# A gated linear unit in float32: two-row tiles in two slots, or one-row tiles in six

## The chip, the cores and the metric

The kernel runs on one core of a Trainium2 chip. A core has a matrix engine (TensorE, not used here), VectorE (DVE), ScalarE (ACT), GpSimd (POOL) and SyncE (SP), a scratch memory (SBUF) of 128 partitions, and 16 DMA engines that carry data between SBUF and the chip's main memory (HBM). DMAs are issued here from two queues: the loads from SP, the stores from ACT. The metric is the device time of one execution in microseconds; a kernel is run several times and the median counts. The profile is of one further execution.

## The reference

```python
def setup_inputs():
    return {"x": np.random.randn(8192, 8192).astype(np.float32)}

def reference(x):
    a, b = np.split(x, 2, axis=-1)
    return a * (1 / (1 + np.exp(-b)))
```

Each row of 8192 numbers (32 KiB) is cut into a front half `a` and a back half `b` of 4096 each. The output row is `a * sigmoid(b)`, 4096 numbers (16 KiB). So 268.4 MB are read, 134.2 MB are written, and each output needs one sigmoid and one product.

## The kernel before

A tile is 128 partitions with two rows each: 64 KiB in and 32 KiB out for each partition, 8 MiB and 4 MiB in all, and 32 tiles cover the input. In HBM, four neighbouring rows belong to one partition: two of them go with an even tile, the other two with the odd tile that follows (`"(g p h r) m -> g h p (r m)"`). A partition's share of a tile is thus one contiguous run, and the runs of two neighbouring partitions start 128 KiB apart in the input and 64 KiB in the output.

SBUF holds two input buffers `x_sb` and two output buffers `o_sb`; tile i uses those of number i % 2.

The work on a tile goes in this order:

1. `load(i)` (line 63) issues the load on SP. It waits for the multiplications of tile i - 2, which read that buffer.
2. `work` (lines 82 to 84) runs the sigmoid on ACT, in place over the back halves, and then the product into `o_sb`. A tile in the middle is cut into two pieces by columns: the first 768 columns of both rows (the list `few_and_most`) are multiplied on POOL, the other 3328 on DVE. The first and the last tile are cut into four pieces, all multiplied on DVE.
3. `store(i)` (line 68) issues the store on ACT, behind the sigmoids, and waits for the products. Before ACT begins the sigmoid of tile i, it also waits until the store of tile i - 2 has landed, because that store frees the output buffer (`by_sigmoid`).

After the work on tile i the program issues the load of tile i + 2 and then the store of tile i. The first tile is loaded and stored in two rows, so that work can begin early; the last one is stored in three pieces.

Each instruction passes through `place`, which keeps the program's order on its engine and drops every dependency except those it is given. Tile's framework adds one kind of wait of its own: DMAs take eight semaphores in turn, and a DMA waits until the earlier one on its semaphore has landed.

Two functions rewrite the finished program at its ends. `_launch_early` puts the first load ahead of the start barrier. `_close_on_sync` lets SP wait for the last store while POOL clears the semaphores. The change leaves both as they are.

Of the kernel before, what the change touches and what calls it, by code (L numbers as in the profile page):

```python
# [8 lines left out]
def _tiles(ctx, tc, x, out):  # L9
    nc = tc.nc  # L10
    P = nc.NUM_PARTITIONS
    DEP = mybir.DependencyInfo(mybir.DependencyClass.Sync, mybir.DependencyReason.DATA)
    fp32 = mybir.dt.float32
    SIG = mybir.ActivationFunctionType.Sigmoid

    n_rows, n_cols = x.shape
    half = n_cols // 2
    R = 2
    SLOTS = 2
    n_tiles = n_rows // (P * R)  # L20
    x_g = x.rearrange("(g p h r) m -> g h p (r m)", p=P, h=2, r=R)
    out_g = out.rearrange("(g p h r) m -> g h p (r m)", p=P, h=2, r=R)

    pool = ctx.enter_context(tc.tile_pool(name="io", bufs=1))
    xs = [pool.tile([P, R * n_cols], fp32, name=f"x_sb{k}") for k in range(SLOTS)]
    os = [pool.tile([P, R * half], fp32, name=f"o_sb{k}") for k in range(SLOTS)]

    whole = [(0, 8)]
    rows = [(0, 4), (4, 8)]
    cut = half // 16 * 3  # L30
    few_and_most = [(0, 8, 0, cut), (0, 8, cut, half)]
    fourths = [(k, k + 2, k % 4 * half // 4, (k % 4 + 2) * half // 4) for k in range(0, 8, 2)]
    loads = [whole] * n_tiles
    works = [few_and_most] * n_tiles
    stores = [whole] * n_tiles
    behind = [0] * n_tiles
    loads[0] = stores[0] = rows
    works[0] = works[-1] = fourths
    stores[-1] = [(0, 4), (4, 6), (6, 8)]
    behind[-1] = 1  # L40

    def meet(a, b):
        return a[0] < b[1] and b[0] < a[1]

    traced = [[] for _ in range(SLOTS)]
    load_of, mul_of, store_of = {}, {}, {}

    def place(i, ins, *needs):


        kept = {n.ins.name for n in needs}
        for e in traced[i % SLOTS]:
            if e.ins.name not in kept:
                tc.declare_no_dep(ins.ins, e.ins, reason="follows from the waits that are kept")
        traced[i % SLOTS].append(ins)
        tc.keep_in_program_order(ins)
        return ins

    def load(i):
        for lo, hi in loads[i]:  # L60
            c = slice(lo * n_cols // 4, hi * n_cols // 4)
            free = [m for w, m in mul_of.get(i - SLOTS, []) if meet(w, (lo, hi))]
            ins = nc.sync.dma_start(out=xs[i % SLOTS][:, c], in_=x_g[i // 2, i % 2, :, c])  # L63
            load_of.setdefault(i, []).append(((lo, hi), place(i, ins, *free)))

    def store(i, lo, hi):
        c = slice(lo * half // 4, hi * half // 4)
        ins = nc.scalar.dma_start(out=out_g[i // 2, i % 2, :, c], in_=os[i % SLOTS][:, c])  # L68
        done = [m for w, m in mul_of[i] if meet(w, (lo, hi))]
        store_of.setdefault(i, []).append(((lo, hi), place(i, ins, *done)))  # L70

    def work(i, lo, hi, near, far):

        rows = xs[i % SLOTS].rearrange("p (r h m) -> p r h m", r=R, h=2)
        packed = os[i % SLOTS].rearrange("p (r m) -> p r m", r=R)
        r, c = slice(lo // 4, (hi + 3) // 4), slice(near, far)
        b = rows[:, r, 1, c]
        landed = [s for w, s in load_of[i] if meet(w, (lo, hi))]
        gone = [s for w, s in store_of.get(i - SLOTS, []) if meet(w, (lo, hi))]
        by_sigmoid = 0 < i < n_tiles - 1  # L80
        needs = [*landed, *(gone if by_sigmoid else ())]
        sig = place(i, nc.scalar.activation(out=b, in_=b, func=SIG), *needs)  # L82
        engine = nc.gpsimd if far == cut and i > 1 else nc.vector
        mul = engine.tensor_mul(out=packed[:, r, c], in0=rows[:, r, 0, c], in1=b)  # L84
        if by_sigmoid:
            for s in gone:
                tc.add_manual_dep(sig.ins, s.ins.name, DEP, reason="frees the output slot")
        place(i, mul, sig, *(() if by_sigmoid else gone))
        mul_of.setdefault(i, []).append(((lo, hi), mul))

    for i in range(SLOTS):
        load(i)
    for i in range(n_tiles):
        due = list(stores[i])
        for k, piece in enumerate(works[i]):
            work(i, *piece)
            ready = works[i][k - behind[i]][1] if k >= behind[i] else 0
            while len(stores[i]) > 1 and k < len(works[i]) - 1 and due[0][1] <= ready:
                store(i, *due.pop(0))
        if i + SLOTS < n_tiles:  # L100
            load(i + SLOTS)
        for lo, hi in due:
            store(i, lo, hi)


def _launch_early(nc):
# [68 lines left out]
@with_exitstack  # L175
def kernel(
    ctx: ExitStack,
    tc: tile.TileContext,
    x: bass.AP,
    out: bass.AP,  # L180
):
    nc = tc.nc
    with ExitStack() as pools:
        _tiles(pools, tc, x, out)
    tc.close()
    tc.compile()
    _launch_early(nc)
    _close_on_sync(nc)
# [30 lines left out]
```

## Time and profile before

| | |
|---|---|
| runs | 932.68 us median of 3 (932.6 to 932.75) |
| the profiled execution's span | 931.1 us |
| loads | 33 DMAs: 31 of 8 MiB, 2 of 4 MiB |
| stores | 35 DMAs: 30 of 4 MiB, 3 of 2 MiB, 2 of 1 MiB |
| from issue to landing, median | 43.5 us for a load, 43.6 us for a store |
| ACT waits for stores to land (line 82) | 630.0 us in 29 waits |
| SP waits for DVE's products (line 63) | 855.5 us in 30 waits |

The span is the profile's time from the first instruction to the end of the last transfer; what a run takes beyond it lies around the program. In the lines of the profile, `q1` is the queue of the loads and `q10` that of the stores; behind the name stand packets, megabytes and the share of the 16 DMA engines' time. A row of the timeline has start, duration, engine, line, operation, output and input, and in brackets how long the engine had been idle and who ended that. A group of instructions has its count, the busy microseconds, the mean nanoseconds of one, and the idle time before.

### The profile page before, as it was taken

To read this page: it belongs to the slowest core of one execution; us is meant where nothing else is said; L and a number is where in the kernel's file an instruction comes from. 1 tells how busy PE (TensorE), PEld (TensorE's weight loads), DVE (VectorE), ACT (ScalarE), POOL (GpSimd) and SP (SyncE) were. 2 spreads that over 40 slices of the span, in tenths; PEclk is the share of its full clock that TensorE was granted. 3 is DMA by queue.
4 is the path that set the end of the run, shared out by engine and by line. 5 is a ranking of instruction groups with operands and counts; after the bars stand their busy time and mean duration, and the time that the engine had idled before them with its cause. 6 is when DMAs were issued, how large, how long until landed. Compare 5 with 4: busy or idle time off the path is not lost.

```text
span 931.1 us, 325 instructions
## 1 busy us (share of the span) xinstructions
DVE 232.5 (25%) x39; ACT 229.8 (25%) x69; POOL 99.9 (11%) x33
## 2 busy tenths in 40 slices
DVE  1133311333113331133320333203332033320233
ACT  2123332033320333203332023320233302333023
POOL 0001111011110111101111011110111101111010
DMA  9999999999999999999999999999999999999998
GB/s 405 450 439 417 428 450 424 455 405 428 450 428 450 407 469 409 428 450 427 452 405 450 428 428 450 424 452 408 428 450 428 450 408 465 411 428 450 427 452 383
DMA packets 9793, 402.67 MB, mean 432 GB/s; under 512 B 1088, under 2 KB 1088, under 8 KB 1088
## 3 DMA queue, kind: packets, MB, share of 16 engines
q1 hardware_dynamic: 4752, 268.44, 66.6%
q10 hardware_dynamic: 5040, 134.22, 33.4%
q14 instruction: 1, 0.01, 0.0%
HBM read 268.44 MB, written 134.22 MB: 432 GB/s over the span
## 4 chain that ended last, share of the span: by engine, by line
DMA 75%; DVE 12%; ACT 12%; issue 0%; ACTq 0%; SPq 0%
DMA out_dram<-o_sb 65%; DVE o_sb L84 12%; ACT x_sb L82 12%; DMA x_sb<-in_x_dram 10%; ACTq L68 0%; SPq L63 0%
## 5 line engine op out<-in xcount | busy, mean ns | idle before, releaser
L84 DVE TENSOR_TENSOR o_sb<-x_sb 128x6656 f32<-128x6656 f32 (+2 forms) x39 | 232.5, 5970 | 690.2 <-ACT x_sb L82 690.2
L82 ACT ACTIVATE x_sb<-x_sb 128x1536 f32<-128x1536 f32 (+1 forms) x68 | 228.5, 3407 | 689.9 <-DMA out_dram<-o_sb 630.0
L84 POOL TENSOR_TENSOR o_sb<-x_sb 128x1536 f32<-128x1536 f32 x29 | 99.7, 3437 | 787.7 <-ACT x_sb L82 787.7
L82 ACT ACT_TABLE_LOAD x1 | 1.3, 1283 | 0.8 <-PEq L203 0.8
L203 POOL MEMSET const-float32-0.0<- 128x1 f32 x1 | 0.1, 98 | 0.2 <-issue 0.2
L203 POOL MEMSET const-bfloat16-1.0<- 128x1 bf16 x1 | 0.1, 101 | 0.0
L203 POOL MEMSET const-uint8-127<- 128x1 uint8 x1 | 0.1, 101 | 0.0
L203 POOL MEMSET const-float32-1.0<- 128x1 f32 x1 | 0.1, 98 | 0.0
## 6 DMA issues: line engine op xcount, KB each, us to landing
out_dram<-o_sb ACTq DMA_DIRECT2D x30, 4096.0 KB, 43.6
x_sb<-in_x_dram SPq DMA_DIRECT2D x2, 4096.0 KB, 16.4
out_dram<-o_sb ACTq DMA_DIRECT2D x3, 2048.0 KB, 28.0
out_dram<-o_sb ACTq DMA_DIRECT2D x2, 1024.0 KB, 8.3
x_sb<-in_x_dram SPq DMA_DIRECT2D x31, 43.5
```

The lines of the kernel that those rows point to most:

```text
L82: sig = place(i, nc.scalar.activation(out=b, in_=b, func=SIG), *needs)
L84: mul = engine.tensor_mul(out=packed[:, r, c], in0=rows[:, r, 0, c], in1=b)
L203: nc = _bacc.Bacc("TRN2", target_bir_lowering=False, num_devices=1)
```

## The change

A tile becomes one row for each partition: 64 tiles with 32 KiB in and 16 KiB out for each partition. Four neighbouring rows still belong to one partition; they now go to four tiles that follow each other. There are six slots of 32 KiB for each partition and no output buffers: the product overwrites the front half of the tile, and the store reads it there. A slot is therefore free when its store has landed, and `load(i)` waits for the store of tile i - 6. DVE does all the products. A tile is one sigmoid, one product and one store; the first and the last tile are cut into two halves by columns, each with a store of its own. Six loads are placed ahead of the first work. The first load is as large as before (4 MiB), but is now the whole first tile.

```diff
-    R = 2
-    SLOTS = 2
-    n_tiles = n_rows // (P * R)
-    x_g = x.rearrange("(g p h r) m -> g h p (r m)", p=P, h=2, r=R)
-    out_g = out.rearrange("(g p h r) m -> g h p (r m)", p=P, h=2, r=R)
+    SLOTS = 6
+    n_tiles = n_rows // P
+    x_g = x.rearrange("(g p r) m -> g r p m", p=P, r=4)
+    out_g = out.rearrange("(g p r) m -> g r p m", p=P, r=4)
...
-    xs = [pool.tile([P, R * n_cols], fp32, name=f"x_sb{k}") for k in range(SLOTS)]
-    os = [pool.tile([P, R * half], fp32, name=f"o_sb{k}") for k in range(SLOTS)]
+    xs = [pool.tile([P, n_cols], fp32, name=f"x_sb{k}") for k in range(SLOTS)]
...
+    ends = {0, n_tiles - 1}
...
     def load(i):
-        for lo, hi in loads[i]:
-            c = slice(lo * n_cols // 4, hi * n_cols // 4)
-            free = [m for w, m in mul_of.get(i - SLOTS, []) if meet(w, (lo, hi))]
-            ins = nc.sync.dma_start(out=xs[i % SLOTS][:, c], in_=x_g[i // 2, i % 2, :, c])
-            load_of.setdefault(i, []).append(((lo, hi), place(i, ins, *free)))
+        ins = nc.sync.dma_start(out=xs[i % SLOTS], in_=x_g[i // 4, i % 4])
+        load_of[i] = place(i, ins, *store_of.get(i - SLOTS, ()))
...
-    def work(i, lo, hi, near, far):
+    def work(i, near, far):
...
-        engine = nc.gpsimd if far == cut and i > 1 else nc.vector
-        mul = engine.tensor_mul(out=packed[:, r, c], in0=rows[:, r, 0, c], in1=b)
...
+        a = xs[i % SLOTS][:, near:far]
+        b = xs[i % SLOTS][:, half + near : half + far]
+        sig = place(i, nc.scalar.activation(out=b, in_=b, func=SIG), load_of[i])
+        mul = place(i, nc.vector.tensor_mul(out=a, in0=a, in1=b), sig)
+        ins = nc.scalar.dma_start(out=out_g[i // 4, i % 4, :, near:far], in_=a)
+        store_of.setdefault(i, []).append(place(i, ins, mul))
+
+    def pieces(i):
+        return [(0, half // 2), (half // 2, half)] if i in ends else [(0, half)]
 
     for i in range(SLOTS):
         load(i)
     for i in range(n_tiles):
-        due = list(stores[i])
-        for k, piece in enumerate(works[i]):
+        for piece in pieces(i):
             work(i, *piece)
...
         if i + SLOTS < n_tiles:
             load(i + SLOTS)
-        for lo, hi in due:
-            store(i, lo, hi)
```

More of the change, by code (lines that the diff above doesn't have):

```diff
@@ L17, in _tiles @@
     half = n_cols // 2
-    R = 2
-    SLOTS = 2
-    n_tiles = n_rows // (P * R)
-    x_g = x.rearrange("(g p h r) m -> g h p (r m)", p=P, h=2, r=R)
-    out_g = out.rearrange("(g p h r) m -> g h p (r m)", p=P, h=2, r=R)
-    pool = ctx.enter_context(tc.tile_pool(name="io", bufs=1))
-    xs = [pool.tile([P, R * n_cols], fp32, name=f"x_sb{k}") for k in range(SLOTS)]
-    os = [pool.tile([P, R * half], fp32, name=f"o_sb{k}") for k in range(SLOTS)]
[L28 to L43, printed above, removed]
+    SLOTS = 6
+    n_tiles = n_rows // P
+    x_g = x.rearrange("(g p r) m -> g r p m", p=P, r=4)
+    out_g = out.rearrange("(g p r) m -> g r p m", p=P, r=4)
+    pool = ctx.enter_context(tc.tile_pool(name="io", bufs=1))
+    xs = [pool.tile([P, n_cols], fp32, name=f"x_sb{k}") for k in range(SLOTS)]
+    ends = {0, n_tiles - 1}
     traced = [[] for _ in range(SLOTS)]
-    load_of, mul_of, store_of = {}, {}, {}
+    load_of, store_of = {}, {}
     def place(i, ins, *needs):
@@ L59, in load @@
     def load(i):
-        for lo, hi in loads[i]:
-            c = slice(lo * n_cols // 4, hi * n_cols // 4)
-            free = [m for w, m in mul_of.get(i - SLOTS, []) if meet(w, (lo, hi))]
-            ins = nc.sync.dma_start(out=xs[i % SLOTS][:, c], in_=x_g[i // 2, i % 2, :, c])
-            load_of.setdefault(i, []).append(((lo, hi), place(i, ins, *free)))
[L66 to L70, printed above, removed]
-    def work(i, lo, hi, near, far):
[L74 to L82, printed above, removed]
-        engine = nc.gpsimd if far == cut and i > 1 else nc.vector
[L84 to L89, printed above, removed]
+        ins = nc.sync.dma_start(out=xs[i % SLOTS], in_=x_g[i // 4, i % 4])
[9 more added lines that the diff above has]
+        return [(0, half // 2), (half // 2, half)] if i in ends else [(0, half)]
     for i in range(SLOTS):
@@ L93, in _tiles @@
     for i in range(n_tiles):
-        due = list(stores[i])
-        for k, piece in enumerate(works[i]):
+        for piece in pieces(i):
             work(i, *piece)
-            ready = works[i][k - behind[i]][1] if k >= behind[i] else 0
-            while len(stores[i]) > 1 and k < len(works[i]) - 1 and due[0][1] <= ready:
-                store(i, *due.pop(0))
         if i + SLOTS < n_tiles:
             load(i + SLOTS)
-        for lo, hi in due:
-            store(i, lo, hi)
 def _launch_early(nc):
```

## The prediction

> **What bounds the kernel now.** I read the page first, its slices and queues, then the queues again for three stretches of the span.
>
> ```profile
> span 931.1 us, 325 instructions
> DVE 232.5 (25%) x39; ACT 229.8 (25%) x69; POOL 99.9 (11%) x33
> ...
> DMA  9999999999999999999999999999999999999998
> ...
> HBM read 268.44 MB, written 134.22 MB: 432 GB/s over the span
> ...
> DMA out_dram<-o_sb 65%; DVE o_sb L84 12%; ACT x_sb L82 12%; DMA x_sb<-in_x_dram 10%; ACTq L68 0%; SPq L63 0%
> ```
>
> No engine is busy for more than a quarter of the span; the transfers are, in every slice. The chain of waits charges 24% to DVE and ACT. That is misleading: it names who released whom, and while DVE multiplies tile i the 16 DMA engines carry other tiles. What counts is whether they ever pause. So the queues, from 100 to 883 us (27 tiles), from 3 to 11 us (loads of one row alone) and from 24 to 45 us (64 KiB load packets beside 16 KiB store packets):
>
> ```profile
> DMA packets 7777, 339.75 MB, mean 434 GB/s; under 512 B 864, under 2 KB 864, under 8 KB 864
> ...
> q1 hardware_dynamic: 3888, 226.49, 66.7%
> q10 hardware_dynamic: 3888, 113.25, 33.5%
> ```
> ```profile
> q1 hardware_dynamic: 102, 3.34, 96.7%
> ```
> ```profile
> q1 hardware_dynamic: 112, 7.34, 81.0%
> q10 hardware_dynamic: 108, 1.77, 19.6%
> ```
>
> In the steady stretch the shares add to 100.2%: the DMA engines never rest, and neighbouring packets overlap by a hair. A packet is one partition's contiguous run: 31 of the 33 loads give 128 of 64 KiB each. Leaving out 432 semaphore packets per queue (864 under 512 B), 3456 loads took 66.7% of 16 x 783 us, 2.418 us each, and the stores of 32 KiB 1.214 us. From the second stretch a 32 KiB load packet takes 0.967 x 8 x 16 / 102 = 1.213 us, from the third a 16 KiB store packet 0.196 x 21 x 16 / 108 = 0.610 us. So 32 KiB more cost 1.205 us (27.2 GB/s for one engine, 435.1 for 16), and every packet has about 8 ns on top, of which some 4 ns overlap with its neighbour (the 0.2%). At 435.1 GB/s all 402.65 MB take 925.4 us. The span is 5.7 us longer: start, packet costs and end are all there is to win.
>
> Last, the work of one tile in the timeline and the shapes of the instructions:
>
> ```profile
> 99.66 7.12 ACT L82 ACTIVATE x_sb<-x_sb 128x1536 f32<-128x1536 f32 x2 [21.82 <-DMA out_dram<-o_sb]
> 101.22 3.44 POOL L84 TENSOR_TENSOR o_sb<-x_sb 128x1536 f32<-128x1536 f32 x1 [25.51 <-ACT x_sb L82]
> 106.81 7.09 DVE L84 TENSOR_TENSOR o_sb<-x_sb 128x6656 f32<-128x6656 f32 x1 [21.85 <-ACT x_sb L82]
> 113.99 0.35 ACTq L68 DMA_DIRECT2D out_dram<-o_sb  x1
> 128.66 7.12 ACT L82 ACTIVATE x_sb<-x_sb 128x1536 f32<-128x1536 f32 x2 [21.88 <-DMA out_dram<-o_sb]
> ```
> ```profile
> L84 DVE TENSOR_TENSOR o_sb<-x_sb 128x6656 f32<-128x6656 f32 x30 | 212.8, 7092 | 634.8 <-ACT x_sb L82 634.8
> L82 ACT ACTIVATE x_sb<-x_sb 128x6656 f32<-128x6656 f32 x30 | 172.0, 5733 | 0.0
> ...
> L84 DVE TENSOR_TENSOR o_sb<-x_sb 128x2048 f32<-128x2048 f32 x8 | 18.0, 2288 | 35.8 <-ACT x_sb L82 35.8
> L82 ACT ACTIVATE x_sb<-x_sb 128x2048 f32<-128x2048 f32 x8 | 14.8, 1901 | 38.9 <-DMA x_sb<-in_x_dram 37.6 <-DVE o_sb L84 1.3
> ```
>
> Tiles start every 29.00 us. That is the DMA engines' time: one of them serves 8 partitions of a tile, 8 load and 8 store packets in turn, 8 x (2.418 + 1.214 - 0.008) + 2 x 0.009 for the semaphore packets = 29.01. (The 9 ns are from the packet records in the trace, which also show load and store packets alternating one by one, on one engine without a pause from 1.0 us to 930.8.)
>
> **The change, part by part.** The bytes stay: 268.44 MB in, 134.22 MB out.
>
> *Packets.* Tiles of one row halve every packet and double their number: loads 32 KiB, stores 16 KiB. One pair takes 1.213 + 0.610 - 0.008 = 1.815 to 1.817 us (the records have 0.611 for the store), a tile 8 x 1.8165 + 0.018 = 14.55 us, two tiles 29.10 against 29.01: 0.094 us more per old tile, 32 of them **+3.0 us**. Bounds: were no overlap left, 8 x 1.824 + 0.018 = 14.61, +0.21 x 32 = +6.9 us; were the cost of a packet proportional to its bytes, 0; were it hidden altogether, -3.0. I take +3.0, since both packet sizes stand in the trace with their durations. The load pattern isn't new either: the two loads of the old tile 0 are this row, of 32 KiB every 128 KiB; they land 9.70 us apart.
> The Trainium skill, "DMA: Bandwidth & Descriptors", section on why small descriptors are slow, gives a fixed overhead of about 3 cycles for each packet, at the 850 MHz of its section on where 436 GB/s comes from. As an estimate, 558 more packets on each engine (semaphores too) would cost 2.0 us by it, against 3.0 by the rows; the trace's 8 ns of duration, about 4 net, are slightly more than its 3.5 ns.
>
> *Multiplication and sigmoid.* POOL loses its 29 multiplications (99.7 us), all beside other work: no gain. DVE takes all. Between 2048 and 6656 elements the rows rise by 1.0425 ns each on DVE and 0.832 on ACT, so 4096 take 4.42 and 3.60 us. DVE has 62 x 4.42 + 4 x 2.29 = 283 us, ACT about 231; neither nears the span. ACT runs sigmoid, waits for DVE, issues the store (0.35): 8.4 us a tile, out of 14.55. What is queued behind that wait is the next sigmoid; 6.1 us of cover remain, so it costs nothing. If the cover were gone, each microsecond over 14.55 would cost 64.
>
> *Slots and waits.* A load now waits for the store of six tiles before (until now for DVE's and POOL's multiplications two tiles before), and the next loads stand behind it on SP. In the built program the DMAs share eight semaphores, so from the sixth on a load also waits for an earlier DMA on its own; about four loads stay in flight. Six slots hold 6 x 14.55 = 87.3 us; one tile needs 14.55 to load beside stores, 8.4 of work and 14.55 to store, 38 us with landing. The other 49 are spent standing in queues: neither runs dry in the middle. Cost 0. The new waits for store landings (0.5 us after the last packet) lie behind that too. 62 more issues of 0.35 us split over SP and ACT; ACT's are in the 8.4, and SP is idle.
>
> *Start.* The first load is again 4 MiB, launched as early, first packet at 1.0 us: 0.
>
> *End.* Before, the last load landed at 911.64 and the stores left over kept the DMA engines busy to the end: no pause. After, let the last load land at T. The last tile's halves are issued at T + 1.9 + 2.3 = T + 4.2 and, after 0.35 + 1.9 + 2.3, at T + 8.75. The store before was issued at T - 6.1. If only it is left, 4.6 of its 8 packets, that is 2.8 us: the DMA engines pause 2.4 us before the first half (1.0 from issue to first packet, as load 0 shows) and 2.1 before the second, **4.5**. If a whole store more is queued, 16 packets x 0.607 = 9.7 us, and 2.45 for the first half: no pause. I expect nearly that, because tile 0's store, in two halves of 8 KiB packets, takes 16 turns against 16 load packets: two rows are loaded meanwhile, and the stores stay about one behind. I take **+0.5**.
>
> Sum: 931.1 + 3.0 + 0.5 = 934.6. The median of the runs is 932.68, 1.56 above the profiled span; kept, that gives **936.2 us**.
>
> **The rivals.**
> *No change* (0.09): the 0.3% between 434 and 435.1 GB/s might go with bytes and not with packets, and the end might be seamless: 932.7 to 934. Against it: the 8 ns come out alike from 64, 32 and 16 KiB packets.
> *Faster* (0.04): the share of the chain charged to compute is real in this one place, that a queue with one load ahead can't let packets overlap fully; with four loads ahead the packet costs vanish. It decides if the pair falls below 1.812 us, half of the old one. All 3.0 us then go: 929.7. Against: the DMA engines already have both queues filled at every turn.
> *Contention* (0.08): when 16 KiB stores first joined, the packet records show load packets of 2.48, 2.49 and 2.44 us on an engine, then 2.418 again. If the new mix, with twice the turns, kept such a 3% on loads (two thirds of the time), +18 us; half of it 945. Each 0.01 us on a 32 KiB packet costs 8 x 64 x 0.01 = 5.1 us. Against: it lasted three packets.
> *Each DMA costs its own gap* (0.05): 62 more at 0.36 us of issue are +22, with the packets 958. Against: 27 tiles with 54 DMAs ran at 100.2%.
> The Trainium skill speaks for a larger price: "SBUF — State Buffer", section on the setup-cost knee, gives every transfer a fixed 2 us or so, an estimated 124 us for 62 more if nothing covered them. The trace disagrees for queued ones: 68 such prices would be 136 us, and the span has 5.7 above its bytes.
>
> **Chances.** Forecast 0.74, its own range 934.5 to 939.5 (pause 0 to 4.5). The measurement tells 0.2%, 1.9 us, from no change. Faster 0.04; within 0.09 and 0.01 of the forecast's lower edge, 0.10; slower 0.86. The range, 933.5 to 942, takes in half of no change and the lighter cases of contention, and leaves out about 2 in 10.
>
> **What would show it.** Right: shares of the two queues still adding to about 100%, 14.55 us between tiles, 18,700 packets of 32 and 16 KiB at 1.213 and 0.611 us, the waits of ACT for loads and SP for stores long but harmless, a pause of at most a few us after the last load. Wrong: a period off 14.55 (packet cost or contention), slices below 9 in the middle (a dry queue), or a long tail.

## The result, and the profile after

The changed kernel takes 936.42 us (median of 4 runs, 936.08 to 936.54), against 932.71 for the kernel before (median of 4): a ratio of 1.0040, 95% interval 1.0028 to 1.0051. It is slower by 3.7 us, where 3.5 were forecast. The profiled execution took 934.8 us, where the sum said 934.6.

The page of the changed kernel, its span, busy times, slices, chain and issues:

```profile
span 934.8 us, 392 instructions
...
DVE 283.5 (30%) x66; ACT 233.1 (25%) x67; POOL 0.2 (0%) x4
...
DMA  9999999999999999999999999999999999999999
...
HBM read 268.44 MB, written 134.22 MB: 431 GB/s over the span
...
DMA x_sb<-in_x_dram 54%; DMA out_dram<-x_sb 35%; DVE x_sb L50 5%; ACT x_sb L49 4%; SPq L42 0%; ACTq L51 0%
...
x_sb<-in_x_dram SPq DMA_DIRECT2D x64, 4096.0 KB, 46.3
out_dram<-x_sb ACTq DMA_DIRECT2D x62, 2048.0 KB, 32.8
```

The chain changed its look entirely: DVE and ACT fell from 24% of it to 9%. The time rose all the same. So the chain's share for compute was no reserve; the row that mattered is the one of the slices, full before and after.

Its queues from 100 to 883 us:

```profile
DMA packets 15513, 338.75 MB, mean 433 GB/s; under 512 B 1728, under 2 KB 1728, under 8 KB 1728
...
q1 hardware_dynamic: 7756, 225.84, 66.8%
q10 hardware_dynamic: 7754, 112.89, 33.7%
```

Twice the packets, and 433 GB/s for 434. The shares add to 100.5% instead of 100.2%, because there are twice as many places where one packet overlaps the next by some 4 ns. By the trace's records of single packets, the bytes carried between 100 and 880 us went at 433.87 GB/s before and 432.52 after. For all 402.65 MB that is 928.05 and 930.95 us: **2.9 us in the middle**.

The groups of instructions by shape, the waits of SP's queue (microseconds in total, times, longest), and rows of the timeline near the end:

```profile
L50 DVE TENSOR_TENSOR x_sb<-x_sb 128x4096 f32<-128x4096 f32 x62 | 274.4, 4425 | 619.4 <-ACT x_sb L49 619.4
L49 ACT ACTIVATE x_sb<-x_sb 128x4096 f32<-128x4096 f32 x62 | 224.2, 3616 | 667.5 <-DMA x_sb<-in_x_dram 667.5
```
```profile
SPq L42 <- DMA out_dram<-x_sb: 760.5, 58, 22.3
SPq L42 <- DMA x_sb<-in_x_dram: 89.7, 30, 20.2
```
```profile
863.08 3.62 ACT L49 ACTIVATE x_sb<-x_sb 128x4096 f32<-128x4096 f32 x1 [10.93 <-DMA x_sb<-in_x_dram]
866.73 4.42 DVE L50 TENSOR_TENSOR x_sb<-x_sb 128x4096 f32<-128x4096 f32 x1 [10.12 <-ACT x_sb L49]
877.68 0.34 ACTq L51 DMA_DIRECT2D out_dram<-x_sb  x1
...
906.73 3.62 ACT L49 ACTIVATE x_sb<-x_sb 128x4096 f32<-128x4096 f32 x1 [10.94 <-DMA x_sb<-in_x_dram]
...
921.27 1.91 ACT L49 ACTIVATE x_sb<-x_sb 128x2048 f32<-128x2048 f32 x1 [10.93 <-DMA x_sb<-in_x_dram]
...
930.19 0.34 ACTq L51 DMA_DIRECT2D out_dram<-x_sb  x1
```

The products took 4.425 us and the sigmoids 3.616, close to the interpolated 4.42 and 3.60. SP now waits for stores (760.5 us) and ACT for loads, at no cost. From 906.73 to 921.27 is one tile, 14.54 us. The store at 877.68 shows one thing more: its product was done at 871.15. It waited 6.5 us for the semaphore that it shares with an earlier load, whose last part landed at 877.60. The trace has five such stores; the transfers already queued cover them.

After the last load landed at 921.27, the last store was issued 8.9 us later, and most DMA engines paused before its packets, for 0.3 us at most and 0.1 on average. The window rows (DMA share last but one) show it:

```profile
921.00:930.00 9.00, 4.42 (x2) 3.82 (x2) 0.00 (x0) 1.00 1.00 426
930.00:931.00 1.00, 0.16 (x1) 0.00 (x0) 0.00 (x0) 1.00 0.88 369
931.00:932.00 1.00, 0.00 (x0) 0.00 (x0) 0.00 (x0) 1.00 1.02 426
```

### The profile page after: what moved, and what is told of

The parts are those of the page before. It is cut to its first block, busy times and chain, and to the rows that moved or that the text cites. A ratio compares the mean times of both kernels' runs of the same rounds, so it can differ in the third digit from the quotient of the medians.

```text
span 934.8 us, 392 instructions
## 1 busy us (share of the span) xinstructions
DVE 283.5 (30%) x66; ACT 233.1 (25%) x67; POOL 0.2 (0%) x4
## 4 chain that ended last, share of the span: by engine, by line
DMA 90%; DVE 5%; ACT 4%; issue 0%; SPq 0%; ACTq 0%
DMA x_sb<-in_x_dram 54%; DMA out_dram<-x_sb 35%; DVE x_sb L50 5%; ACT x_sb L49 4%; SPq L42 0%; ACTq L51 0%
## 5 line engine op out<-in xcount | busy, mean ns | idle before, releaser
L50 DVE TENSOR_TENSOR x_sb<-x_sb 128x4096 f32<-128x4096 f32 (+1 forms) x66 | 283.5, 4296 | 646.6 <-ACT x_sb L49 646.6
L49 ACT ACTIVATE x_sb<-x_sb 128x4096 f32<-128x4096 f32 (+1 forms) x66 | 231.8, 3513 | 693.9 <-DMA x_sb<-in_x_dram 688.4
```

Source lines behind the costliest of these rows:

```text
L50: mul = place(i, nc.vector.tensor_mul(out=a, in0=a, in1=b), sig)
```

## The experiments

The theory: DMA engines that never rest pay for each packet, whatever its size, and besides that only pauses at the ends count. The rivals: each DMA brings a gap of its own; or the slots, the in-place product, DVE alone and the new waits cost it. "Middle" is the time for all 402.65 MB at the rate carried between 100 and 880 us, from the packet records. The kernel before ran again beside every group of these kernels, with medians from 932.62 to 932.74 us.

| kernel | time, us | ratio to before (95%) | middle, us |
|---|---|---|---|
| before | 932.7 | | 928.05 |
| after | 936.42 | 1.0040 (1.0028 to 1.0051) | 930.95 |
| halved packets | 935.34 | 1.0030 (1.0019 to 1.0042) | 930.44 |
| two DMAs by row | 936.64 | 1.0043 (1.0028 to 1.0058) | 930.97 |
| three big slots | 936.01 | 1.0036 (1.0023 to 1.0050) | 928.16 |
| 4 KiB packets | 964.66 | 1.0344 (1.0328 to 1.0359) | 955.67 |
| big slots, last stores in quarters | 934.05 | 1.0016 (1.0006 to 1.0025) | 928.21 |
| first tile whole | 938.16 | 1.0059 (1.0044 to 1.0074) | 930.96 |
| four slots | 938.40 | 1.0061 (1.0046 to 1.0076) | 930.96 |
| doubled product | 936.19 | 1.0038 (1.0024 to 1.0052) | 930.94 |
| two slots | 1137.19 | 1.218 (1.213 to 1.223) | (paused) |

**Only the packets halved.**

```diff
 # the kernel before
-    x_g = x.rearrange("(g p h r) m -> g h p (r m)", p=P, h=2, r=R)
+    x_g = x.rearrange("(g p r h) m -> g h p r m", p=P, h=2, r=R)
-    out_g = out.rearrange("(g p h r) m -> g h p (r m)", p=P, h=2, r=R)
+    out_g = out.rearrange("(g p r h) m -> g h p r m", p=P, h=2, r=R)
...
```

The lines left out (...) let `load` and `store` address the two rows of a tile separately, each DMA as large as before.

> The kernel before, its two slots, 68 DMAs and POOL unchanged; only which two rows make a tile differs (rows 0 and 2, 1 and 3 of each four), so every load packet is 32 KiB instead of 64 and every full store packet 16 KiB instead of 32. Packet theory (each packet costs about 4.5 ns net whatever its size, a semaphore packet 9 ns): 488 more data packets on each DMA engine, no more semaphores, +2.2 us, 934.9. Theory that each DMA brings its own gap: no more DMAs, 932.7. Theory that slots, in-place products or waits cost it: unchanged, 932.7.

935.34 us, +2.7. Its queues from 100 to 880 us:

```profile
DMA packets 14580, 337.54 MB, mean 433 GB/s; under 512 B 842, under 2 KB 842, under 8 KB 842
...
q1 hardware_dynamic: 7290, 224.92, 66.7%
q10 hardware_dynamic: 7289, 112.61, 33.7%
```

The semaphore packets (under 512 B) stayed as few as before, the data packets doubled, and two thirds of the change's cost came back without any of its slots or waits. In the middle it is 930.44 - 928.05 = 2.39 us for 488 packets on each DMA engine: 4.9 ns each, a little over the 4.5 assumed. The other 0.3 lies at the start, where load packets run longer (0.4 us more for each DMA engine than in the kernel before, by the packet records).

**The same packets as twice the DMAs.**

```diff
 # the kernel before
-    loads = [whole] * n_tiles
+    loads = [rows] * n_tiles
     works = [few_and_most] * n_tiles
-    stores = [whole] * n_tiles
+    stores = [rows] * n_tiles
-    behind = [0] * n_tiles
+    behind = [1] * n_tiles
-    loads[0] = stores[0] = rows
+    behind[0] = 0
```

> The kernel before with every load and store split into its two rows: packets as in the changed kernel, and nearly its number of DMAs (64 loads, 65 stores), but two slots and POOL as before. Packet theory: 488 data packets at 4.5 ns and 61 semaphore packets at 9 ns more on each DMA engine, +2.7 us, 935.4. Theory that each DMA brings its own gap and packets nothing: the whole of the change's cost, 936.4, and 0.6 us or less between this and the kernel with halved packets would speak against it. Theory that slots or waits cost it: 932.7.

936.64 us, +4.0: a miss by 1.2, and by the time alone this looks like the gap theory. The middle says otherwise: 0.53 us more than with halved packets, for 61 semaphore packets on each DMA engine, 8.7 ns each; a semaphore packet lasts 9. The remainder is at the end: most DMA engines finish near 933.5 us, the slowest at 935.1, against 0.6 us of spread before. Why is open.

**The changed manner with the old packets.** No output buffers, products into the slot, DVE alone, loads waiting for stores, as in the changed kernel; the second row's product is written right behind the first's, so that a store is one run for each partition.

```diff
 # the changed kernel
-    SLOTS = 6
-    n_tiles = n_rows // P
+    R = 2
+    SLOTS = 3
+    n_tiles = n_rows // (P * R)
...
+        to = t[:, r * half + near : r * half + far]
+        return place(i, nc.vector.tensor_mul(out=to, in0=a, in1=b), sig, *before)
...
+            m = [work(i, 0, 0, half)]
+            m.append(work(i, 1, 0, half, *m))
+            store(i, 0, 2 * half, *m)
...
```

> The changed kernel's manner (no output buffers, products into the slot, DVE alone, a load waits for the landing of the store that frees its slot) with two rows in a tile and three slots of 64 KiB: the packets and the 68 DMAs of the kernel before. Packet theory: 932.7, within 0.5. Theory that slots freed by stores, in-place products or DVE alone cost the change its time: 936.4 or more.

936.01 us: a miss, and at first sight the structure theory's number. But the middle is that of the kernel before (928.16), and the window rows show where 3 us went:

```profile
918.00:921.00 3.00, 2.09 (x1) 3.00 (x3) 0.00 (x0) 1.00 0.83 360
921.00:924.00 3.00, 3.00 (x3) 1.66 (x2) 0.00 (x0) 1.00 0.00 0
924.00:927.00 3.00, 2.84 (x2) 1.73 (x1) 0.00 (x0) 1.00 1.04 437
```

From 921 to 924 nothing is carried. The last load landed at 916.97 (before: at 911.64), so fewer stores were left to cover the work on the last tile. The next kernel changes only that end.

```diff
 # the three big slots, the last tile
-            m = [work(i, 0, 0, h), work(i, 0, h, half)]
-            m.append(work(i, 1, 0, h, *m))
-            store(i, 0, half, *m[:2])
...
+            for r in range(2):
+                for near in (0, h):
+                    m.append(work(i, r, near, near + h, *m[:2]))
+                    if len(m) > 1:
+                        store(i, (len(m) - 2) * h, (len(m) - 1) * h, m[-2])
+            store(i, 3 * h, 4 * h, m[-1])
```

> The three big slots again (936.01 us, against 932.7 expected), with only the last tile's stores changed: four stores of 1 MiB, each issued as soon as its product is done, instead of one of 2 and two of 1 MiB. In the trace of the three big slots the steady rate is that of the kernel before, and the DMA engines pause 3 us, from 921 to 924, because the first store of the last tile is issued only 6.9 us after the last load landed. Theory that this pause is all that the structure costs: the first store comes at 4.2 us instead, the pause shrinks to 1.2 us or less, and the four stores end about 2.4 us earlier: 933.6. Theory that in-place products, DVE alone or loads waiting for stores cost the rest in the middle: 936 again.

934.05 us, 2.0 less. Its window over the same 3 us:

```profile
921.00:924.00 3.00, 2.84 (x3) 2.22 (x2) 0.00 (x0) 1.00 0.75 306
```

A pause of 0.8 us is left (0.25 x 3). So in-place products, DVE alone and loads that wait for stores cost the middle no more than 0.2 us together (928.21 against 928.05), and this is the fastest variant with slots freed by stores; it doesn't reach the kernel before.

**Packets of 4 KiB.** A gap in SBUF after every 4 KiB cuts the runs; the rows in HBM, the DMAs, the slots and the work stay as in the changed kernel.

```diff
 # the changed kernel
-    xs = [pool.tile([P, n_cols], fp32, name=f"x_sb{k}") for k in range(SLOTS)]
+    RUN, GAP = 1024, 16
+    xs = [pool.tile([P, n_cols // RUN * (RUN + GAP)], fp32, name=f"x_sb{k}") for k in range(SLOTS)]
+    xs = [t.rearrange("p (k c) -> p k c", c=RUN + GAP)[:, :, :RUN] for t in xs]
...
```

> The changed kernel with a gap of 64 bytes in SBUF after every 4 KiB, so that a partition's run is cut into packets of 4 KiB; DMAs, slots, waits and work stay. On each DMA engine a tile has 64 load and 32 store packets instead of 8 and 8: 5120 more in all. Packet theory: at 4.5 ns net each +23 us, 959.5 (at 8 ns, were no overlap left, 977). Theories of a gap for each DMA, or of slots and waits: 936.4.

964.66 us, 28.2 more than the changed kernel. Its queues from 100 to 880 us:

```profile
DMA packets 81899, 328.66 MB, mean 421 GB/s; under 512 B 1664, under 2 KB 1664, under 8 KB 81896
...
q1 hardware_dynamic: 54280, 218.93, 68.2%
q10 hardware_dynamic: 27616, 109.71, 34.2%
```

Over five times the packets, and the middle takes 24.7 us more, for 5120 packets on each engine: 4.8 ns each. The other 3 to 4 us are pauses at the end (952 to 955 and 958 to 960). Pairs of kernels with packets from 4 to 64 KiB give the same price, so it goes with the packet and not with bytes or DMAs. As only the SBUF side is cut here, it isn't a matter of where the rows lie in HBM either. By the time this was a miss by 5: of it 1.7 us are the price above the assumed 4.5 ns, the rest the end.

**The backlog at the end.**

```diff
 # the changed kernel
-    ends = {0, n_tiles - 1}
+    ends = {n_tiles - 1}
```

> The changed kernel with the first tile in one piece, one store of 16 KiB packets instead of two of 8 KiB. The prediction said that the two half stores put the store queue about one store behind, and that this backlog covers the end. If so, this kernel has less queued when the last load lands, and pauses up to 4.5 us instead of 0.3: 938 to 941. If the backlog comes from elsewhere, the end stays as it was: 936.4, less 0.1 for eight packets.

938.16 us, 1.7 more, from removing one DMA at the other end of the kernel. Its last load landed at 923.90, 2.6 us later than in the changed kernel, and its end pauses (window rows):

```profile
928.00:930.00 2.00, 0.14 (x1) 1.45 (x1) 0.00 (x0) 1.00 0.67 283
930.00:932.00 2.00, 1.51 (x1) 0.46 (x1) 0.00 (x0) 1.00 0.77 315
932.00:934.00 2.00, 0.79 (x1) 0.00 (x0) 0.00 (x0) 1.00 0.21 86
```

The missing shares are about 0.7, 0.5 and 1.6 us. That the way the first tile is stored sets this, 900 us earlier, can be followed in the packet records. Take as backlog the output of the rows already loaded that isn't stored yet, in stores of 2 MiB, averaged over the 14.55 us of a tile. In the changed kernel it is 2.77 from 75 us on and still 2.77 from 905 us on; here it is 2.23 and 2.36.

**Fewer slots.**

```diff
 # the changed kernel
-    SLOTS = 6
+    SLOTS = 4
```

> The changed kernel with four slots instead of six. Theory that the DMA engines' packets set the pace and the queues never run dry: four slots hold 58.2 us of DMA time, a tile needs 38, so the middle stays at 14.55 us a tile: 936.4, within 1 for the end. Theory that the landing of stores, for which the loads wait, is what costs time: two slots fewer make every load wait longer, and the time grows by several us or more.

938.40 us: the middle is unchanged (930.96), so four slots keep the queues as full as six. The 2 us, more than the 1 allowed for, are a pause of 1.9 us from 930.9 to 933 at the end (window rows):

```profile
930.00:932.00 2.00, 2.00 (x1) 0.00 (x0) 0.00 (x0) 1.00 0.45 188
932.00:934.00 2.00, 0.05 (x1) 0.00 (x0) 0.00 (x0) 1.00 0.61 258
```

The backlog explains it. Up to 45 us it is that of the changed kernel (2.48 and 2.49 from 30 us on); by 75 us it is 2.39, with four slots, and stays so to the end; what four slots change in between is open. The missing 0.38 of a store is 3 packets of 0.61 us on each DMA engine, 1.9 us in all. With two slots:

> The changed kernel with two slots. By the prediction's sum a tile needs 38 us from the issue of its load to the landing of its store when both transfers share the DMA engines, and 25.5 when they don't (10.7 load, 8.4 work, 6.4 store); two slots give it 29.1 at full pace. Theory that slots matter only through the queues running dry: now they do, the DMA engines pause while both tiles are worked on, slices fall below 9, and the time is clearly above 960, at most 64 x 19 = 1216. Theory that the landings of the stores, for which loads wait, cost nothing even now: 936 to 940.

1137.19 us. The slices of its page:

```profile
DMA  9989889898898998889989899898998989889897
GB/s 369 360 342 374 347 351 360 349 370 343 351 371 350 368 353 350 353 350 368 353 349 361 343 369 350 344 360 351 367 353 350 363 343 375 343 351 369 351 369 296
```

Here the queues do run dry, and 17.7 us pass for a tile. This is how a real lack of slots looks: slices of 8 among those of 9, and 355 GB/s. The pauses are not all of it: of the 200 us more than in the changed kernel, the packet records put 117 on each DMA engine into pauses and 84 into load packets that last longer than 1.213 us.

**Compute doubled.**

```diff
 # the changed kernel
         mul = place(i, nc.vector.tensor_mul(out=a, in0=a, in1=b), sig)
+        if 0 < i < n_tiles - 4:
+            mul = place(i, nc.vector.tensor_mul(out=a, in0=a, in1=b), mul)
```

> The changed kernel with a second multiplication by the sigmoid in the tiles 1 to 59 (so 59 tiles give a times the square of the sigmoid); the first and the last four tiles are as before, so that the end stays. DVE has 4.42 us more in each of them, ACT's wait for it grows as much: 12.9 us a tile of 14.55. Theory that compute is hidden: 936.4. Theory by the chain of waits, which charges 5% of the span to DVE: its share doubles, about +46 us; were DVE's whole time on the path, 59 x 4.42 = +261.

936.19 us and a middle of 930.94: 261 us more work on DVE, and nothing lost.

## Why the prediction was right

*Packets, +3.0.* Measured 2.9 in the middle. The price was read from durations that stood in the old trace (8 ns of duration less some 4 of overlap) and is 4.8 to 4.9 ns in three kernels, 8.7 for a semaphore packet. Kernels with the same packets have middles up to 0.16 us apart, so the price is known to about 0.3 ns, that of a semaphore packet only to 2 or 3. The step's own arithmetic is slightly off: 29.10 less 29.01 is 0.09 us, or +2.9 for 32 tiles, and its upper bound comes to +6.7 instead of +6.9. The bounds weren't needed: the overlap stayed some 4 ns for each packet. The Trainium skill, "DMA: Bandwidth & Descriptors", section on why small descriptors are slow, names about 3 cycles for each packet (an estimate of 3.5 ns at its 850 MHz); the runs have it 1.3 ns dearer, and just as independent of size.

*Multiplication and sigmoid, 0.* The doubled product shows that at least 4.4 of the 6.1 us of cover were there.

*Slots and waits, 0.* The middles with six and with four slots agree to 0.01 us. The prediction named the shared semaphores; it didn't say that stores too would stand behind loads (five times, some 6 us), which cost nothing here.

*End, +0.5.* The pause was 0.3 us at most. The reason given, that the half stores of the first tile keep the store queue behind, is shown by the kernel without them; that the number of slots sets the backlog too was not in the sum. The size was chosen between the two ends worked out, 0 and 4.5, so its coming so near is luck in part: with the first tile whole or with four slots the pause is 2.5 or 2.0 us on average. "About one behind" was a rough size: by the queues from 921.27 us on, 5.11 MB were left, 2.1 of them the last tile's, so 3.0 MB or 11.5 packets a DMA engine where the sum had up to 16. With 11.5, its own figures give 7.0 + 2.45 = 9.4 us of cover for the 8.9 + 1.0 until the last store's first packet: a pause of 0.5.

*Start, 0.* Not quite: load packets beyond their usual duration cost each DMA engine 1.3 us in the first 80 us after the change and 1.0 before. With 2.9 in the middle, 0.3 here and 0.1 of pause at the end, the last packets come 3.4 us later on the mean of the 16 DMA engines, as the records have it. The other 0.3 of the 3.6 us between the spans is that the slowest engine ends 0.1 further behind this mean and that the last landing took 0.2 longer. Why load packets run longer at the start is open.

*The rivals.* No change and faster fell with the packet price. Contention stayed at the start, as in the old trace; there it was more than the three packets that the prediction counted on one engine: others have load packets of up to 2.86 us when the stores join at 21 us, and single ones of up to 2.51 again at 70 us. A gap for each DMA is refuted in the middle: 61 more DMAs cost 0.53 us, 8.7 ns each. The Trainium skill, "SBUF — State Buffer", section on the setup-cost knee, gives each transfer some 2 us; with work queued behind it, no run here shows that price.

Where the expectations missed (three big slots, two DMAs by row, 4 KiB packets, four slots), the middle came as the packet price has it and the end was not counted. The one step to do better is to sum the end for every kernel as was done for the changed one.

## What to carry to other kernels

In these kernels, where the shares of the DMA queues add to 100%, compute and waits in the middle of the run were worth nothing, whatever the chain charged to them; count packets (contiguous runs for each partition), at about 5 ns each here, and keep them long. Then look only at what the DMA engines carry after the last load has landed: enough stores must be queued there to cover the last tile's work. Buffers beyond those that keep the queues filled buy nothing in the middle, but they can leave more stores queued for the end: six slots instead of four were worth 2.0 us here, all of it there.

## What the runs showed that was not expected

With two slots a load's packets behind a pause last longer: the first of the eight 32 KiB packets on an engine takes 1.79 us on the mean instead of 1.213, while the store packets stay at 0.611. The fifth, sixth and eighth are long too (1.35, 1.64, 1.37), mostly without a pause before them, so a pause isn't the whole reason; the rest is open. Long first packets (1.8 us) also stand at the start of the kernels before and after.

The queue q14, which the profile calls `instruction`, moves 8 KiB in 0.31 us each time on the same DMA engines: in the kernel before once before the last transfer, in the changed kernel three times. Each time one engine has a gap of 0.30 us between its data packets and, beside it, a load packet that is 0.25 to 0.53 us longer than usual. The last engine to finish sets the end, and in the changed kernel two of the 16 finish 0.3 us or more behind the others. That these are the ones delayed in this way is not shown: the records have no engine numbers, and which packets belong to one engine is read from where one ends and the next begins.
